# A hybrid decoder block: four edits where the retention stage begins

## The chip, the core and the metric

The kernel runs on one core of one Trainium2 chip. A core has a tensor engine for matrix products (PE, with its weight loads shown apart as PEld), a vector engine (DVE), a scalar engine (ACT), GpSimd (POOL), and a queue engine (SP) that mostly issues DMA transfers. Each engine works through its own list of instructions in order; semaphores order the engines among themselves. The metric is device time in microseconds (us). The kernel before took 2226.19 us, the median of three runs (2223.69 to 2228.32).

## The reference

One decoder block for one sequence of 1024 tokens of width 1024, all in float32:

```python
mod = jax.nn.silu(c) @ w_ada[l] + b_ada[l]
sh1, sc1, g1, sh2, sc2, g2 = jnp.split(mod, 6, axis=-1)
h = modulate(rms_norm(x, norm1_g[l]), sh1, sc1)
x = x + g1[:, None, :] * token_mixer(h, ...)
h = modulate(rms_norm(x, norm2_g[l]), sh2, sc2)
x = x + g2[:, None, :] * squared_relu_mlp(h, w_ff1[l], w_ff2[l])
return rms_norm(x, norm_f_g)
```

The token mixer projects `h` to queries, keys, values and gates. One branch is a chunkwise retention with 4 heads (256 channels for queries and keys, 512 for values) over 8 chunks of 128 tokens:

```python
s = jnp.einsum('bhid,bhjd->bhij', qi, ki) * inner_decay[None]
o = (jnp.einsum('bhij,bhje->bhie', s, vi)
     + jnp.einsum('bhid,bhde->bhie', qi, state) * q_decay[None, :, :, None])
state = (state * chunk_decay[None, :, None, None]
         + jnp.einsum('bhjd,bhje->bhde', ki * k_decay[None, :, :, None], vi))
```

Its output is normalized per head, scaled, multiplied by `silu(rg)` and projected. The other branch is a dilated sliding-window attention. The two are merged by sigmoid gates and projected once more.

## The kernel before, in words

Every product is made in float32 by splitting each operand into a high part and a low part and summing three matmuls (`mm3`, lines 201, 203 and 205: low weights by high data, high by low, high by high). So a product has the shape "128 by 128 weights, 128 by 512 data, three times". ACT usually makes the high part (a copy) and DVE the low part (a subtraction).

The stages follow each other: modulation and first norm; the attention values (`av`); queries, keys and gates (`queries_keys`); the retention values (`values`); retention (`chunk`, once per head and chunk, 32 times); attention; the output projections; the MLP. What surrounds the change is the end of `values`, the first chunks of retention, and the opening of attention.

**Values.** `values` goes through 14 steps of four parts `p`. Each part's matmuls are followed, one part later, by `v_post`, which finishes a result on ACT and DVE and stores it to device memory (`vd`, line 1070). The last but one step makes the tiles `vo12p` (lines 1061 and 1062), the last makes `vr1p` (lines 1066 to 1068; `vr10`, `vr11`, `vr12`, `vr13` by part). In the last but one step `values` also prepares the first two chunks' rotated queries and keys, `jit_qk(0)` and `jit_qk(1)`, and calls `ahead(2)` once. In the last step POOL queues eight reloads of halves of `hh` and `hl` (lines 1099 and 1100). Then it opens retention's memory (`open_ret`) and fetches values and queries and keys of the next two chunks.

**Retention.** A chunk `g` has these parts, in this order on PE: the score product `sT` and the transposes `kT` (`s_kt`, made one chunk ahead, the first two in chunk 0), the state's increments `kv` (two, from `kh`, `kl` and the values), the output `o` (from the state's halves `sh`, `sl` and the scores), the transposes `oT` of the previous chunk's normalized output, and between them pieces of the gate projection `rg`. `s_kt` copies the scores out with ACT into a small tile `sm` (line 638), multiplies by the decay and splits them (lines 639 to 642), then makes `kh` and `kl` (lines 648 and 649). The state is updated on DVE (lines 703 and 705) and split into `stateh` and `statel` (lines 719 and 720). `o` is normalized on DVE with a detour over POOL (`bn`, `ba`, `gr`, `onm`, lines 729 to 735); `onm` is the last reader of `o`. `jit_qk(i)` splits the fetched queries and keys of chunk `i` into `j`: a copy on ACT (line 615) and a subtraction on POOL (line 616). The products other than `rg` rotate over four banks of PSUM, so that a new product waits for the last reader of an earlier one; `kT` of the third chunk, for one, takes the bank of the first chunk's `o`.

**Loads in order.** `Steps` holds a list of steps, each with loads that a helper turns into operands. Loads are issued on SP in the order of the list, at most three ahead of those used, into three buffers `raw`. `ahead(n)` prepares the loads of the following step: `split_w` for weights (lines 191 and 192), and `mod_prep` for one column of the later modulations (a DVE product with a sum, line 455, and an addition, line 457). Each chunk's step holds one modulation load, each second one a weight load before it.

**Memory.** The pools are stacks: a pool opened where another was closed lies on the same bytes, and within a pool each kind of tile gets its place when its first tile is made. A new tile waits for the last users of whatever lay on its bytes, DMA stores among them. Retention's pool lies on the pool of the stages before, which has 26 tiles of 4 KB for each partition. Its kinds are the state, then values `V`, queries and keys `qk`, the small tiles `sm`, `smh`, `sml`, `kh`, `kl`, the split operands `j`, the tiles `bn` to `on`, and the 12 tiles of 4 KB of the kind "E" (`etile`, line 524), which hold each head's transposed outputs `on{h}{e}` and gates `srg{h}{e}`. Before the change the first E tile is made in `on_T` in chunk 1, so the E tiles lie behind all others.

**The opening of attention.** In `att_step(0, 0)` the last head is finished: `u_final` (line 663) scales each of its four `on` tiles on ACT (line 670), multiplies by `srg` on DVE (line 672) and stores to `y` (line 673). `result_sums` queues sums of `y` on POOL. Then `open_att` closes retention's pool and opens attention's, on the same bytes. `q_prep` makes `qh` and `ql` (lines 1209 and 1210) and `k_split` makes `kh` and `kl` of the first attention head from the projection `ak` (lines 1218 and 1219); the scores `sc` need all four, and stand on PE between pieces of the next `ak`:

```python
hi, lo = ring(f"kh{pair}{g}{a}"), ring(f"kl{pair}{g}{a}")
src, h_, l_ = by_blocks(ps, g), shaped(hi, g), shaped(lo, g)
nc.scalar.copy(h_, src)
nc.vector.tensor_sub(l_, src, fv(h_))
```

Of the kernel before, what the change touches and what calls it, by code (L numbers as in the profile page):

```python
# [134 lines left out]
def block_kernel(ctx, tc, io, stop=None, dbg=None):  # L135
# [3 lines left out]
    def fv(t):  # L139
        return t.bitcast(F32)  # L140
# [56 lines left out]
    def mm3(outs, w, xs, first, last, skip=False):  # L197

        wh, wl = w
        for o, (xh, xl) in zip(outs, xs):  # L200
            nc.tensor.matmul(o, wl, xh, start=first, stop=False, skip_group_check=skip)  # L201
        for o, (xh, xl) in zip(outs, xs):
            nc.tensor.matmul(o, wh, xl, start=False, stop=False, skip_group_check=skip)  # L203
        for o, (xh, xl) in zip(outs, xs):
            nc.tensor.matmul(o, wh, xh, start=False, stop=last, skip_group_check=skip)  # L205
# [246 lines left out]
    def mod_prep(i):  # L452

        def prep(raw):
            nc.vector.scalar_tensor_tensor(raw, raw, 1.0, cb, op0=ALU.mult, op1=ALU.mult,
                                           accum_out=mods[:, i:i + 1])
            nc.vector.tensor_add(mods[:, i:i + 1], mods[:, i:i + 1], vec[:, VC_BADA + i:VC_BADA + i + 1])
        return prep

    def mod_load(i):  # L460
        return io["w_ada"][i], mod_prep(i)
# [19 lines left out]
    def proj_mm(ps, w, ks=range(NK)):  # L481
        outs = ps if isinstance(ps, list) else [ps[:, 0, :], ps[:, 1, :]]
        for k in ks:
            mm3(outs, wk(w, k), hx[k], k == 0, k == NK - 1)
# [32 lines left out]
    def open_ret():  # L517
# [3 lines left out]
        R["sh"] = R["p"].tile([P, 2, DV], F32R, name="stateh")  # L521
        R["sl"] = R["p"].tile([P, 2, DV], F32R, name="statel")

    def etile(name, dt=F32):
        return R["p"].tile([P, 1024], dt, tag="E", bufs=12, name=name)

# [54 lines left out]
    hd = {}  # L581
    NG = H * NC
# [25 lines left out]
    def jit_qk(i):  # L608
        src = hd["qk", i]
        if i > 1:  # L610
            t = R["p"].tile([P, 2, 4, C], F32R, tag="j", bufs=2, name=f"j{i}")
        else:
            t = whl.tile([P, 1024], F32R, tag=("wh", "wl")[i], name=f"j{i}")
            t = t.rearrange("p (a b c) -> p a b c", a=2, b=4)
        nc.scalar.copy(t[:, 0], src)  # L615
        nc.gpsimd.tensor_sub(t[:, 1], src, fv(t[:, 0]))  # L616
        hd["j", i] = t

    def s_kt(i):

        p = R["p"]
        g = i
        h, c = divmod(g, NC)
        t = hd["j", g]
        ps = ps_s(f"sT{h}{c}")
        for i in range(2):
            nc.tensor.matmul(ps[:, :2 * C], t[:, 0, 2 + i, :], t[:, :, i, :], start=i == 0, stop=False,
                             skip_group_check=True)
            nc.tensor.matmul(ps[:, :C], t[:, 1, 2 + i, :], t[:, 0, i, :], start=False, stop=i == 1,  # L629
                             skip_group_check=True)  # L630
        pk = ps_s(f"kT{h}{c}", (P, 2, P)) if c < NC - 1 else None
        if pk is not None:
            for i in range(2):
                nc.tensor.transpose(pk[:, i, :], hd["qk", g][:, 2 + i], ident)
        sm = p.tile([P, C], F32, tag="sm", bufs=1, name=f"sm{h}{c}")
        smh = p.tile([P, C], F32R, tag="smh", bufs=2, name=f"smh{h}{c}")
        sml = p.tile([P, C], F32R, tag="sml", bufs=2, name=f"sml{h}{c}")
        nc.scalar.copy(sm, ps[:, :C])  # L638
        nc.vector.tensor_add(sm, sm, ps[:, C:2 * C])
        nc.vector.tensor_mul(sm, sm, decay[:, h * C:(h + 1) * C])  # L640
        nc.scalar.copy(smh, sm)
        nc.vector.tensor_sub(sml, sm, fv(smh))
        hd["s", g] = (smh, sml)
        if pk is not None:
            kd = ct[:, CS_KDEC + h:CS_KDEC + h + 1]
            kh = p.tile([P, 2, P], F32R, tag="kh", bufs=1, name=f"kh{h}{c}")
            kl = p.tile([P, 2, P], F32R, tag="kl", bufs=1, name=f"kl{h}{c}")
            nc.scalar.mul(kh, pk, kd)
            nc.vector.scalar_tensor_tensor(flat(kl), flat(pk), kd, fv(flat(kh)), op0=ALU.mult, op1=ALU.subtract)
            hd["k", g] = (kh, kl)  # L650

    def on_T(h, c):

        po = ps_s(f"oT{h}{c}", (P, 4, P))
        on = hd["o", h, c]
        if c == 0:
            hd["on", h] = [etile(f"on{h}{e}") for e in range(4)]
        for e in range(4):
            nc.tensor.transpose(po[:, e, :], on[:, e * P:(e + 1) * P], ident)
        for e in range(4):  # L660
            nc.scalar.copy(hd["on", h][e][:, c * C:(c + 1) * C], po[:, e, :])
# [13 lines left out]
    def chunk(h, c, ahead, w=None):  # L675
        p = R["p"]
        g = NC * h + c
        if g + 3 < NG:
            fetch(g + 3)
        if c % 2 == 0:  # L680
            hd["rgw"] = w
            hd["rgp"] = ps_mm(f"rg{h}{c}")

        ks = {0: (5, 6, 6), 1: (6, 7, 8)}.get(g) or [4 * (c % 2) + i for i in (0, 2, 4)]
        if g == 0:
            proj_mm(hd["rgp"], hd["rgw"], range(2))
            s_kt(0)
            proj_mm(hd["rgp"], hd["rgw"], range(2, 5))
        vh, vl = hd["v", g][:, 0], hd["v", g][:, 1]
        st, sh, sl = R["state"], R["sh"], R["sl"]  # L690
        kvs = []
        if c < NC - 1:
            kh, kl = hd["k", g]
            for i in range(2):
                kv = ps_s(f"kv{h}{c}{i}")
                mm3([kv], (kh[:, i, :], kl[:, i, :]), [(vh, vl)], True, True)
                kvs.append(kv)
        if g == 0:
            s_kt(1)
        proj_mm(hd["rgp"], hd["rgw"], range(*ks[:2]))  # L700
        for i, kv in enumerate(kvs):
            if c == 0:
                nc.vector.tensor_copy(st[:, i, :], kv)
            else:
                nc.vector.scalar_tensor_tensor(st[:, i, :], st[:, i, :], float(GAMMA[h] ** C), kv,
                                               op0=ALU.mult, op1=ALU.add)
        if g > 0:
            ahead(2)
        if 0 < g < NG - 1:
            s_kt(g + 1)  # L710
        po = ps_s(f"o{h}{c}")
        if c > 0:
            t = hd["j", g]
            for i in range(2):
                mm3([po], (t[:, 0, i, :], t[:, 1, i, :]), [(sh[:, i, :], sl[:, i, :])], i == 0, False)
        mm3([po], hd["s", g], [(vh, vl)], c == 0, True)
        if c < NC - 1:
            for i in range(2):
                nc.scalar.copy(sh[:, i, :], st[:, i, :])
                nc.vector.tensor_sub(sl[:, i, :], st[:, i, :], fv(sh[:, i, :]))  # L720
        if g + 2 < NG:
            jit_qk(g + 2)
        if g > 0:
            on_T(*divmod(g - 1, NC))
        proj_mm(hd["rgp"], hd["rgw"], range(*ks[1:]))
        bn = p.tile([P, 6], F32, tag="bn", bufs=2, name=f"bn{h}{c}")
        ba = p.tile([P, 2], F32, tag="ba", bufs=2, name=f"ba{h}{c}")
        gr = p.tile([P, 1], F32, tag="gr", bufs=2, name=f"gr{h}{c}")
        nc.vector.bn_stats(bn, po)
        nc.vector.bn_aggr(ba, bn)  # L730
        nc.vector.tensor_scalar(gr, ba[:, 1:2], ct[:, CS_QD2 + h:CS_QD2 + h + 1], GN_EPS, op0=ALU.mult, op1=ALU.add)
        nc.gpsimd.tensor_tensor(gr, gr, mhalf[:, 0:1], op=ALU.pow)
        nc.vector.tensor_mul(gr, gr, ct[:, CS_QD + h:CS_QD + h + 1])
        on = p.tile([P, DV], F32, tag="on", bufs=1, name=f"onm{h}{c}")
        nc.vector.tensor_scalar(on, po, ba[:, 0:1], gr, op0=ALU.subtract, op1=ALU.mult)
        hd["o", h, c] = on
        if g == 0:
            ahead(2)
        if c % 2 == 1:
            hd["srg", h, c // 2] = etile(f"srg{h}{c // 2}")  # L740
            nc.scalar.activation(hd["srg", h, c // 2], flat(hd["rgp"]), AF.Silu)
        if h > 0 and c < 4:
            u_final(h - 1, (c,))

    def wsplit(ap):
        return ap, split_w
# [368 lines left out]
    later_mods = [G1 + k for k in range(NK)] + [SH2 + k for k in range(NK)] + \  # L1115
                 [SC2 + k for k in range(NK)] + [G2 + k for k in range(NK)]

    for h in range(H):
        for c in range(NC):
            steps.add((lambda h, c: lambda ahead, *w: chunk(h, c, ahead, *w))(h, c),  # L1120
                      ([wsplit(io["w_rg"][4 * h + c // 2])] if c % 2 == 0 else []) + [mod_load(later_mods[8 * h + c])],
                      manual=True)


# [1334 lines left out]
```

## Time and profile before

| what | value |
|---|---|
| median of three runs | 2226.19 us (2223.69 to 2228.32) |
| the profiled execution | 2226.56 us; span from first to last instruction 2224.8 us |
| PE busy | 2177.1 us (98%) |
| DVE, ACT, POOL busy | 1454.5 us (65%), 907.3 us (41%), 145.5 us (7%) |
| mean granted clock of PE | 0.997 |
| bytes moved by DMA | 408.93 MB, 184 GB/s over the span |

The profile is one execution on the chip. Its page gives busy times by engine, the span in 40 slices, the chain of work that ended last, and groups of instructions. The trace behind it can be asked for the instructions of a stretch in order of time, for who waited for whom, and for busy times in windows. A row of the timeline has the start and the duration in us, the engine, the line of the kernel, the operation, the tile written and the tiles read, the shapes, a count where equal instructions were merged, and in brackets the idle time of the engine before it with what ended it. Matmuls are pipelined: the next one starts before the one before has ended. SPq is SP's queue; a DMA is shown at its issue, and its landing comes later. A view of the DMAs in a stretch lists issues with their sizes and the median us from issue to landing.

### The profile page before, as it was taken

The page shows a single profiled execution, that of the slowest core. Times are in us where ns is not written, and L with a number is a line of the kernel's source. Part 1 is how long each engine was busy: PE and PEld are TensorE (multiplying, and loading weights), DVE is VectorE, ACT ScalarE, POOL GpSimd, SP SyncE. Part 2 cuts the span into 40 slices and gives each one's busy share as a digit, 9 for nine tenths or more (in the row PEclk, how much of TensorE's full clock was granted, in tenths as well). Part 3 has the DMA queues.
Part 4 walks back from the last instruction along what each step waited for, and adds up shares of the span by engine and source line. Part 5 has one row for each costly group of instructions (what it writes and reads, how often), then busy time and mean ns, then how long its engine had stood idle before and what let it go on. Part 6 is the DMA issues. An engine that isn't in the chain of part 4 may idle for free.

```text
span 2224.8 us, 27161 instructions
## 1 busy us (share of the span) xinstructions
PE 2177.1 (98%) x10130; PEld 1803.4 (81%) x10130; DVE 1454.5 (65%) x2285; ACT 907.3 (41%) x1665; POOL 145.5 (7%) x168
## 2 busy tenths in 40 slices
PE   7999999999999999999999999999999999999998
PEld 4888888888877888888888788888778888888887
DVE  6628777764448778855554644676876665787855
ACT  4323332223434445544534633424454445533412
POOL 0001111000012122100000000002100000000003
PEclk9999999999999999999999999999999999999999
DMA  9539999725775556549813355645144444745322
GB/s 364 200 134 284 299 284 284 200 103 189 250 268 169 167 179 212 188 162 248 235 60 96 105 196 211 237 160 176 62 149 152 149 156 168 261 139 171 122 85 77
DMA packets 154371, 408.93 MB, mean 184 GB/s; under 512 B 27062, under 2 KB 54973, under 8 KB 149822
## 3 DMA queue, kind: packets, MB, share of 16 engines
q1 hardware_dynamic: 148542, 363.14, 46.5%
q0 software_dynamic: 5696, 44.04, 8.4%
q8 instruction: 80, 1.31, 0.2%
q14 instruction: 53, 0.43, 0.1%
HBM read 316.27 MB, written 156.13 MB: 212 GB/s over the span
## 4 chain that ended last, share of the span: by engine, by line
PE 86%; DVE 6%; ACT 3%; DMA 2%; issue 1%; POOL 0%; SPq 0%; POOLq 0%; DVEq 0%; ACTq 0%
PE qap L203 5%; PE qap L201 5%; PE qap L205 5%; PE av L769 4%; PE fp L203 4%; PE fp L201 4%; PE fp L205 4%; PE rg L201 2%; PE rg L203 2%; PE rg L205 2%; PE f2a L203 2%; PE f2a L201 2%; PE f2a L205 2%; PE ak L201 2%; PE ak L203 2%; PE ak L205 2%
## 5 line engine op out<-in xcount | busy, mean ns | idle before, releaser
L201 PE MATMUL qap<-hh,qaw 128*128 128x512 f32 x216 | 84.0, 389 | 0.0
L203 PE MATMUL qap<-hl,qaw 128*128 128x512 f32 x216 | 84.0, 389 | 0.0
L205 PE MATMUL qap<-hh,qaw 128*128 128x512 f32 x216 | 84.0, 389 | 0.0
L616 POOL TENSOR_TENSOR j<-qk,j 128x512 fp32r<-128x512 f32 x32 | 43.3, 1352 | 465.0 <-ACT j L615 465.0
L1918 ACT ACTIVATE a<-a 128x512 f32<-128x512 f32 x48 | 30.3, 632 | 76.2 <-DVE a L1917 76.2
L1272 ACT ACTIVATE P<-P,ng 128x128 f32<-128x128 f32 (+1 forms) x96 | 41.9, 438 | 39.2 <-DVE ng L1269 39.2
L258 DVE TENSOR_TENSOR fw<-w1r,fw 128x512 fp32r<-128x512 f32 x48 | 33.0, 688 | 37.6 <-ACT fw L248 37.6
L1815 POOL TENSOR_TENSOR accnf<-accnf,sqnf 128x256 f32<-128x256 f32 (+1 forms) x18 | 16.6, 922 | 613.5 <-ACT sqnf L1814 613.4
L258 DVE TENSOR_TENSOR qaw<-wa,qaw 128x512 fp32r<-128x512 f32 x54 | 36.0, 685 | 30.9 <-ACT qaw L248 30.9
L2104 ACT CAST w2h<-w2s 128x512 fp32r<-128x512 f32 x36 | 22.4, 621 | 78.1 <-DVE w2s L2142 77.0
L201 PE MATMUL fp<-h2h,fw 128*128 128x512 f32 x128 | 50.0, 390 | 0.0
L203 PE MATMUL fp<-h2l,fw 128*128 128x512 f32 x128 | 49.8, 389 | 0.0
L205 PE MATMUL fp<-h2h,fw 128*128 128x512 f32 x128 | 49.8, 389 | 0.0
L201 PE MATMUL roa<-rh,rwl 128*128 128x512 f32 x128 | 49.8, 389 | 0.0
L203 PE MATMUL roa<-rl,rwh 128*128 128x512 f32 x128 | 49.8, 389 | 0.0
L205 PE MATMUL roa<-rh,rwh 128*128 128x512 f32 x128 | 49.8, 389 | 0.0
L1653 DVE TENSOR_TENSOR rwl<-rwl,rwh 128x1024 fp32r<-128x1024 f32 x25 | 30.2, 1221 | 29.1 <-ACT rwh L1683 29.1
L638 ACT COPY sm<-sT 128x128 f32<-128x128 f32 x32 | 8.5, 266 | 98.8 <-PE sT L629 92.7
L201 PEld LDWEIGHTS qap<-hh,qaw 128*128 128x128 f32 x216 | 40.5, 188 | 8.5
L205 PEld LDWEIGHTS qap<-hh,qaw 128*128 128x128 f32 x216 | 40.5, 188 | 8.4
L203 PEld LDWEIGHTS qap<-hl,qaw 128*128 128x128 f32 x216 | 40.5, 188 | 8.4
L1815 POOL TENSOR_TENSOR accn<-accn,sqn 128x512 f32<-128x512 f32 x12 | 15.5, 1294 | 478.5 <-ACT sqn L1814 478.5
(3081 smaller groups left out, 7181.0 us busy)
## 6 DMA issues: line engine op xcount, KB each, us to landing
v<-vd SPq DMA_DIRECT2D x32, 512.0 KB, 4.9
raw<-in_w_ada_dram SPq DMA_DIRECT2D x32, 512.0 KB, 4.9
w1r<-in_w_ff_dram SPq DMA_DIRECT2D x32, 512.0 KB, 5.0
vd<-vo SPq DMA_DIRECT2D x24, 512.0 KB, 6.5
yt<-y POOLq DMA_DIRECT2D x6, 2048.0 KB, 15.3
xsd<-as SPq DMA_DIRECT2D x24, 512.0 KB, 2.7
w2r<-in_w_ff2s_dram SPq DMA_DIRECT2D x24, 512.0 KB, 7.6
em<-in_w_ada_dram SPq DMA_DIRECT2D x16, 512.0 KB, 10.2
```

The source lines that it names most:

```text
L201: nc.tensor.matmul(o, wl, xh, start=first, stop=False, skip_group_check=skip)
L203: nc.tensor.matmul(o, wh, xl, start=False, stop=False, skip_group_check=skip)
L205: nc.tensor.matmul(o, wh, xh, start=False, stop=last, skip_group_check=skip)
L258: nc.vector.tensor_sub(t[:, 512:], src, fv(t[:, :512]))
L616: nc.gpsimd.tensor_sub(t[:, 1], src, fv(t[:, 0]))
L638: nc.scalar.copy(sm, ps[:, :C])
L769: nc.tensor.matmul(av[g][c], x[k][:, c * C:(c + 1) * C], w[j][:, ws], start=k == 0 and (x, j) == parts[0], stop=k == NK - 1 and (x, j) == ...
L1272: nc.scalar.activation(v, v, AF.Exp, bias=ng[:, blk:blk + 1], accum_out=st[:, g, blk, 2 + a:3 + a])
L1653: nc.vector.tensor_sub(lo, fv(lo), fv(hi))
L1815: (nc.vector if f == 7 else nc.gpsimd).tensor_add(G["acc", key], G["acc", key], sq)
L1918: nc.scalar.activation(o, o, AF.Relu)
L2104: nc.scalar.copy(hi, src)
```

## The change

Four edits, all around the entry of retention. `open_ret` makes the four `on` tiles of head 0 at once, right after the state, and `on_T` no longer makes them for head 0; since these are the first tiles of the kind "E", all 12 E tiles get their place there, ahead of `V`, `qk` and the small tiles. `jit_qk(2)`, which splits the third chunk's rotated queries and keys, is called in chunk 0 right after `s_kt(1)` and not behind the split of the state. The second modulation's load moves from the step of chunk 1 into that of chunk 0, so that `ahead(2)` in `values` prepares both first modulations. In chunk 0 `ahead(2)` is called where all other chunks call it; the next step then holds nothing to prepare.

```diff
@@ open_ret
+        hd["on", 0] = [etile(f"on0{e}") for e in range(4)]
+
@@ on_T
-        if c == 0:
+        if c == 0 and h > 0:
             hd["on", h] = [etile(f"on{h}{e}") for e in range(4)]
@@ chunk
         if g == 0:
             s_kt(1)
+            jit_qk(2)
         proj_mm(hd["rgp"], hd["rgw"], range(*ks[:2]))
...
-        if g > 0:
-            ahead(2)
+        ahead(2)
         if 0 < g < NG - 1:
             s_kt(g + 1)
...
-        if g + 2 < NG:
+        if 0 < g < NG - 2:
             jit_qk(g + 2)
...
         hd["o", h, c] = on
-        if g == 0:
-            ahead(2)
@@ the steps of retention
-                      ([wsplit(io["w_rg"][4 * h + c // 2])] if c % 2 == 0 else []) + [mod_load(later_mods[8 * h + c])],
+                      ([wsplit(io["w_rg"][4 * h + c // 2])] if c % 2 == 0 else []) +
+                      [mod_load(later_mods[8 * h + i]) for i in ({0: (0, 1), 1: ()}.get(8 * h + c, (c,)))],
```

## The prediction

> **The bound.** I read the page, then the waits of the tensor engine, then its timeline where the waits are long.
>
> ```profile
> span 2224.8 us, 27161 instructions
> PE 2177.1 (98%) x10130; PEld 1803.4 (81%) x10130; DVE 1454.5 (65%) x2285; ACT 907.3 (41%) x1665; POOL 145.5 (7%) x168
> ...
> PE 86%; DVE 6%; ACT 3%; DMA 2%; issue 1%; POOL 0%; SPq 0%; POOLq 0%; DVEq 0%; ACTq 0%
> ```
>
> The tensor engine (PE) is busy for 98% of the span and carries 86% of the chain that ended last. A change pays only where PE stands still or runs slowly, and costs only where it makes PE wait. This is the entry of retention in PE's timeline (start, duration, in brackets the idle time before and its releaser):
>
> ```profile
> 661.83 0.61 PE L205 MATMUL rg<-hh,raw_4661h 128*128 128x512 f32 x2
> 664.65 0.54 PE L201 MATMUL kv<-v,kl 128*128 128x512 f32 x1 [2.21 <-DVE kl L649]
> 674.03 0.39 PE L627 MATMUL sT<-j 128*128 128x256 f32 x1 [0.70 <-POOL j L616]
> 675.66 0.44 PE L634 MATMUL kT<-ct,qk 128*128 128x128 f32 x2 [0.95 <-DVE onm L735]
> 677.59 0.50 PE L201 MATMUL o<-stateh,j 128*128 128x512 f32 x1 [1.49 <-DVE state L705]
> 683.20 0.39 PE L201 MATMUL kv<-v,kl 128*128 128x512 f32 x1
> ```
>
> Four stalls, 5.35 us together, between 662.44 (661.83 + 0.61) and the third chunk's first kv at 683.20. The same stretch cut into windows of 3.41 us (busy us and count of PE, PEld, DVE, ACT, POOL, then PE's granted clock, DMA share, GB/s):
>
> ```profile
> 661.55:664.97 3.42, 1.21 (x5) 0.69 (x5) 1.36 (x4) 0.94 (x3) 0.00 (x0) 1.00 1.04 392
> 664.97:668.38 3.41, 3.41 (x13) 2.90 (x12) 0.00 (x0) 0.26 (x1) 0.00 (x0) 0.50 0.80 274
> 671.79:675.21 3.42, 2.22 (x11) 1.47 (x9) 2.62 (x7) 2.05 (x4) 1.86 (x2) 1.00 0.00 0
> 675.21:678.63 3.42, 1.49 (x7) 1.07 (x8) 3.38 (x7) 0.00 (x0) 0.00 (x0) 1.00 0.14 25
> 678.63:682.04 3.41, 3.41 (x12) 2.73 (x11) 2.89 (x8) 0.88 (x3) 0.00 (x0) 0.50 1.03 375
> ```
>
> After a window with PE busy 1.21 or 1.49 us the next is granted half the clock; after one with 2.22 us it is not. A half-speed window full of matmuls loses 3.41 / 2 = 1.7 us. So the entry holds 5.35 + 3.4 = 8.8 us that are not work; that is all a perfect entry could give.
>
> **Small tiles.** The first stall ends with the first chunk's `sm`, on whose chain `kl` and kv hang:
>
> ```profile
> 662.46 0.27 ACT L638 COPY sm<-sT 128x128 f32<-128x128 f32 x1 [6.13 <-DMA vd<-vr]
> 664.12 0.48 DVE L649 SCALAR_TENSOR_TENSOR kl<-kT,ct,kh 128x256 fp32r<-128x256 f32 x1
> ...
> 654.36 8.00 DMA vd<-vr
> ...
> 648.92 8.48 SPq L1070 DMA_DIRECT2D vd<-vr  x4
> ...
> DMA packets 3525, 8.02 MB, mean 388 GB/s; under 512 B 325, under 2 KB 1163, under 8 KB 3523
> ...
> raw<-in_w_ada_dram SPq DMA_DIRECT2D x1, 512.0 KB, 9.3
> ```
>
> `sm` lies where `vr12` lay, whose store (third of four) is issued at 654.36 and lands 8.00 us later. With `on00` to `on03` allocated first, the twelve E tiles come ahead of the small ones, and `sm` lies on `vr10`, the first store, issued at 648.92. A 512 KB load issued 3.5 us before it took 9.3 us, so the first store takes 8.0 to 9.3 and lands at 656.9 to 658.2. From 645.3 to 666 the DMA engines are full (388 GB/s), and the change puts another 512 KB into that (with the modulation): 524 KB / 388 = 1.35 us, up to 2.0 while the reloads of `hh` share the engines. I take the late end, 660.2. `sm` at 660.3 is 2.16 earlier, `kl` ends at 664.60 - 2.16 = 662.44, just when PE is ready: kv at 662.5 instead of 664.65, and no half-speed window behind it. Bounds: nothing, if `vr10` lands as late as `vr12` did; 2.2 + 1.7 = 3.9 at most.
>
> **Third chunk.** `j2` moves ahead of the copies of the state. The rows that set the pace:
>
> ```profile
> 670.17 1.28 DVE L703 COPY state<-kv 128x512 f32<-128x512 f32 x2
> 671.54 1.30 DVE L720 TENSOR_TENSOR statel<-state,stateh 128x512 fp32r<-128x512 f32 x2
> 672.00 0.61 ACT L615 CAST j<-qk 128x512 fp32r<-128x512 f32 x1
> 672.70 1.28 POOL L616 TENSOR_TENSOR j<-qk,j 128x512 fp32r<-128x512 f32 x1 [22.94 <-ACT j L615]
> 674.79 0.81 DVE L735 TENSOR_SCALAR onm<-o,ba,gr 128x512 f32<-128x512 f32 x1
> 675.52 1.22 DVE L455 SCALAR_TENSOR_TENSOR raw<-raw,cb 128x1024 f32<-128x1024 f32 x1
> 676.85 1.28 DVE L705 SCALAR_TENSOR_TENSOR state<-state,kv 128x512 f32<-128x512 f32 x2
> 681.87 0.48 DVE L649 SCALAR_TENSOR_TENSOR kl<-kT,ct,kh 128x256 fp32r<-128x256 f32 x1
> 658.05 0.55 SPq L597 DMA_DIRECT2D qk<-qkd  x1
> qk<-qkd SPq DMA_DIRECT2D x1, 256.0 KB, 7.7
> ```
>
> At full speed two rg take 0.61 and one kv 0.39, so matmuls of 512 columns start 0.22 to 0.23 us apart, six in 1.36. Then kv runs from 662.5 to 663.9, and sT with kT, two such matmuls' columns in six pieces, to about 664.4. From `sm` to the end of `kl` is 664.60 - 662.46 = 2.14: the second `kl` ends at 666.6, the copies of the state at 667.8. PE does rg and o until 666.5, the second kv pair until 668.0, rg until 669.4. `qk02` lands at 658.05 + 7.7 + 1.35 = 667.1, `j2` ends on ACT at 667.7 and on POOL at 669.0: sT at 669.4 no longer waits. That removes the 0.70, and if `qk` is late it costs nothing until 667.5.
>
> But kT needs the bank of `o`, so it waits for `onm`, whose chain is untouched. ACT is held by `j2` until 667.7 and makes `stateh` by 668.3. Then `statel` meets `j2` on POOL, and there are rows for such a meeting: POOL's op beside a VectorE subtraction of two SBUF operands that otherwise takes 1.21.
>
> ```profile
> 637.18 1.21 DVE L1027 TENSOR_TENSOR vwl<-vwl,vwh 128x1024 fp32r<-128x1024 f32 x1
> 639.85 1.29 POOL L616 TENSOR_TENSOR j<-qk,j 128x512 fp32r<-128x512 f32 x1 [0.30 <-ACT j L615]
> 639.90 2.31 DVE L1027 TENSOR_TENSOR vwl<-vwl,vwh 128x1024 fp32r<-128x1024 f32 x1
> ```
>
> It took 2.31, so I let `statel` start when POOL ends, at 669.0 (0 to 1.1 us for this meeting; 0.7 taken). The Trainium skill, page "SBUF — State Buffer", section "SBUF: two separate sides", says that the pair of ports shared by VectorE and GpSimd is an exclusive lock held for a whole instruction; these rows agree. From the start of `statel` to the end of `onm` is 675.60 - 671.54 = 4.06: 673.1. kT starts at 673.15: its stall grows from 0.95 to about 3.2.
>
> **Modulation.** The second modulation (DVE 675.52 to 676.85, 1.33 us, between `onm` and `state`) moves into the values' stage. There it stands before one `vo`, whose store goes out 1.3 later; `v01` now lies on that tile and waits for the store on SP, behind the `vr` stores that are issued until 657.4 anyway, and the queue stays deep enough to hide up to 1 us of a later issue. The matmuls of the last values' step take nothing from it; were that cover gone, it would cost its 1.33. Once it has run, its buffer is free, and the load of a later modulation, 512 KB, goes out in the values' stage instead of in the first chunks: the extra transfer costed above, and one load less on SP in the first chunk. So L705 follows `onm` directly: first half done at 673.75, o at 673.8 instead of 677.59. The third chunk's `kl` ends 681.87 + 0.48 - 676.85 = 5.50 after L705 starts (673.05): 678.55. PE needs 683.20 - 677.59 = 5.61 from o to kv with a half-speed window in it, 5.61 - 1.7 = 3.9 without. The stall of 3.2 will most likely bring one: kv at 679.4; without, it waits for `kl`: 678.6. The entry gives 683.20 - 679.4 = 3.8 us (3.8 to 4.6; with the bounds above 0 to 5.2). Nothing takes it back before the exit, for PE is busy all the way there, at full clock:
>
> ```profile
> 684.00:989.00 305.00, 305.00 (x1481) 253.58 (x1480) 238.70 (x492) 145.93 (x357) 55.49 (x60) 1.00 0.53 175
> ```
>
> **The exit.** When attention opens, its tiles lie on retention's memory from the bottom up. The E tiles were at the top, out of the way; now they are at the bottom. In the changed program `kh010` lies on `on33`, the last tile of retention, and its copy on ACT carries a new wait, on the store of `on33`; before it lay on an old `v`.
>
> ```profile
> 986.32 1.23 DVE L672 TENSOR_TENSOR on<-on,srg 128x1024 f32<-128x1024 f32 x1 [0.18 <-ACT on L670]
> 983.35 4.58 SPq L673 DMA_DIRECT2D y<-on  x4
> 987.13 1.00 ACT L1218 CAST kh<-ak 128x1024 fp32r<-128x1024 f32 x1
> 988.60 1.22 DVE L1219 TENSOR_TENSOR kl<-ak,kh 128x1024 fp32r<-128x1024 f32 x1
> 989.87 0.38 PE L203 MATMUL sc<-kl,qh 128*128 128x256 f32 x1 [0.35 <-DVE kl L1219]
> ...
> y<-on SPq DMA_DIRECT2D x4, 512.0 KB, 2.8
> ```
>
> The store is issued when DVE ends, 987.55, and takes 2.8 or, as the queue fills behind it, a little more: it lands at 990.5. `kh` runs to 991.6, `kl` to 992.9, and PE's second sc starts at 992.95 instead of 989.87: 3.1 us lost (2.8 to 4), since sc waits for `kl` today. Behind `kh` on ACT stand the split of the next weights and the next `qh`; both have a projection's time to spare. PE is idle for 3.4 of 3.8 us, more than the entry's stalls, so I add one half-speed window, 1.7 (0 to 3.4). Sum 4.8. The Trainium skill, "TensorE: Matmul & The Clock Gate", section "What's actually happening", lets the clock fall after an idle window of about 3.4 us; the table agrees on the length, but not that the window must be idle throughout. By this page of the Trainium skill neither stall need bring a half-speed window, and the sum would be -4.6 + 3.1 = -1.5.
>
> **Sum.** -3.8 + 4.8 = +1.0. Their phase is chance, so I weigh in a little of the case without half-speed windows (-4.6 + 3.1 = -1.5) and take +0.7. The profiled execution took 2226.56 us (span 2224.8), 0.37 above the median of the runs, 2226.19: 2226.9 for the median.
>
> **Rivals.** (a) Only the entry counts: the wait of `kh` is hidden, because the store of `on33` lands before ACT comes to `kh`. Then -3.8 to -5.2: 2221.0 to 2222.4. It decides if the store lands by 987.2; against it, the store is issued at 987.55.
>
> (b) Slower: the entry's gain is lost to the DMA queue. Place: `qk02`, `j2`, `stateh`, `statel`, `onm`, one behind the other. Each us that `qk02` lands after 667.1 moves `onm` and o by one; at 670.9 the 3.8 us are gone and the exit's 4.8 stand alone: 2231.0. For it: the queue is full, and 7.7 to 9.3 us deep. Against it: only 512 KB are added, 1.35 us.
>
> (c) The change does not do what it says: `sm` meets another late store and kv stays at 664.65. Then `onm` stays at 675.6, only the 1.3 us of the modulation are won, and the exit costs 4.8: +3.5, 2229.7. Against it: `vr10` is issued 5.4 us before `vr12`.
>
> (d) No half-speed window follows either stall: -1.5, 2224.7. For it: 2.22 busy us in a window did not bring one. Against it: 1.49 did, and both new stalls leave less than that in most positions of the window. The Trainium skill's page on the clock gate, named above, would expect this one.
>
> **Numbers.** The forecast has 0.56, (d) 0.10, (c) 0.05: all within 0.2% (4.5 us, about what a measurement of this kernel can tell from no change). (a) has 0.15; two thirds of it lie beyond -0.2%, 0.10. (b) has 0.14, of which 0.13 beyond +0.2%. Hence faster 0.10, same 0.77, slower 0.13. The likeliest case alone reaches from 2223.5 to 2229.5 (the runs shown spread from 2223.69 to 2228.32); leaving about 0.1 out on each side, 2221.9 to 2230.8.
>
> **Signs.** Right: ACT's `sm` about 2 us earlier and no long wait before the first kv; kT waiting about 3 us for `onm`; the third chunk's kv about 4 us earlier; `kh` (L1219 in the changed file) waiting for the DMA y<-on, a stall of about 3 us before sc, and half clock behind it. Wrong: sc without a stall (a), `j` waiting for `qk` past 668 (b), a first kv at 664.65 (c), full clock throughout (d).

## The result

The changed kernel took 2232.41 us, the median of eight runs (2231.58 to 2234.39); the kernel before took 2226.28 beside it (2223.69 to 2228.87). The ratio is 1.0029, with a 95% interval of 1.0020 to 1.0039: slower by 6.1 us, where 2226.9 had been predicted. The time lies outside the predicted range. The profiled execution took 2232.31 us.

The page of the changed kernel (span, busy time of PE, shares of the chain that ended last):

```profile
span 2230.5 us, 27163 instructions
...
PE 2177.7 (98%) x10130; PEld 1804.1 (81%) x10130; DVE 1455.0 (65%) x2285; ACT 906.5 (41%) x1665; POOL 145.3 (7%) x168
...
PE 84%; DVE 6%; DMA 3%; ACT 3%; issue 1%; POOL 0%; SPq 0%; POOLq 0%; DVEq 0%; ACTq 0%
```

PE's work is the same (2177.7 against 2177.1 us busy). The span is 5.7 us longer, so nearly all of the loss is PE standing still. The page does not say where. The timeline does, read beside the kernel before. First the entry and the exit in the changed kernel:

```profile
660.49 0.27 ACT L640 COPY sm<-sT 128x128 f32<-128x128 f32 x1 [4.30 <-DMA vd<-vr]
662.68 0.50 PE L201 MATMUL kv<-v,kl 128*128 128x512 f32 x1 [0.37 <-DVE kl L651]
672.60 0.44 PE L636 MATMUL kT<-ct,qk 128*128 128x128 f32 x2 [2.18 <-DVE onm L737]
673.29 0.47 PE L201 MATMUL o<-stateh,j 128*128 128x512 f32 x1 [0.25 <-DVE state L708]
678.01 0.50 PE L201 MATMUL kv<-v,kl 128*128 128x512 f32 x1 [0.57 <-DVE kl L651]
978.13 4.58 SPq L675 DMA_DIRECT2D y<-on  x4
985.58 1.01 ACT L1219 CAST kh<-ak 128x1024 fp32r<-128x1024 f32 x1 [3.56 <-DMA y<-on]
986.64 0.39 PE L201 MATMUL sc<-kh,ql 128*128 128x256 f32 x1 [2.46 <-ACT kh L1219]
987.90 0.39 PE L203 MATMUL sc<-kl,qh 128*128 128x256 f32 x1 [0.87 <-DVE kl L1220]
```

The third chunk's kv starts at 678.01 instead of 683.20, and the retention's last stores start at 978.13 instead of 983.35: 5.2 us gained, and kept all through retention. At the exit 2.46 + 0.87 = 3.33 us of stalls stand where there were 0.35; the second sc is still 2.0 us earlier than before (987.90 against 989.87). Up to here the prediction's rows come out, without its half-speed windows: this execution has none at the entry or the exit. What the prediction does not have stands 65 us later, in the attention:

```profile
1050.89 1.05 ACT L191 CAST raw_8402h<-raw 128x1024 fp32r<-128x1024 f32 x1 [4.17 <-DMA raw<-in_w_gate_dram]
1053.35 0.71 PE L201 MATMUL gate<-hh,raw_8402l 128*128 128x512 f32 x2 [0.69 <-DVE raw_8402l L192]
1055.82 1.05 ACT L191 CAST raw_8501h<-raw 128x1024 fp32r<-128x1024 f32 x1 [3.88 <-DMA raw<-in_w_gate_dram]
1058.87 0.36 PE L201 MATMUL sc<-kh,ql 128*128 128x256 f32 x1 [1.18 <-DVE P L1250]
1061.63 0.58 PE L203 MATMUL sc<-kl,qh 128*128 128x256 f32 x1 [2.41 <-DVE kl L1220]
1085.18 0.73 PE L201 MATMUL gate<-hh,raw_8603l 128*128 128x512 f32 x2 [1.01 <-ACT g00s L1539]
```

The weights of two gate projections come late, ACT and DVE fall behind, and PE waits 0.69 + 1.18 + 2.41 = 4.28 us, with a half-speed window (1061.11 to 1064.52) behind it. Before the change, the splits of the same two weights on ACT and the wait of the last row stood here:

```profile
1048.90 1.03 ACT L191 CAST raw_8402h<-raw 128x1024 fp32r<-128x1024 f32 x1
1050.10 1.05 ACT L191 CAST raw_8501h<-raw 128x1024 fp32r<-128x1024 f32 x1 [0.17 <-DMA raw<-in_w_gate_dram]
1080.89 0.73 PE L201 MATMUL gate<-hh,raw_8603l 128*128 128x512 f32 x2 [0.79 <-ACT g00s L1538]
```

So 2.0 us ahead at 988 have become 4.3 behind at 1085. The other 1.4 us of the 5.7 come later; a half-speed window at 1293.21, which the profile of the kernel before does not have, loses about 1.7 there. Why the weights are late is seen in the issues on SP and POOL. Before, where `std<-st` writes 16 KB of the attention's statistics to device memory, `stn<-std` reads them back, and `yt` are the sums of results that `result_sums` puts on POOL's queue:

```profile
989.64 0.60 POOL L566 DMA_DIRECT2D yt<-y  x1 [17.06 <-DMA y<-on]
1022.70 0.62 SPq L1330 DMA_DIRECT2D std<-st  x1
1023.65 1.17 POOL L567 DMA_DIRECT2D yt<-y  x1 [20.78 <-DMA yt<-y]
1027.17 0.37 SPq L1331 DMA_DIRECT2D stn<-std  x1
1028.95 12.10 SPq L85 DMA_DIRECT2D raw<-in_w_gate_dram  x2
```

And after:

```profile
984.40 0.60 POOL L568 DMA_DIRECT2D yt<-y  x1 [17.04 <-DMA y<-on]
1017.72 1.17 POOL L569 DMA_DIRECT2D yt<-y  x1 [20.65 <-DMA yt<-y]
1019.43 0.62 SPq L1331 DMA_DIRECT2D std<-st  x1
1038.39 0.37 SPq L1332 DMA_DIRECT2D stn<-std  x1
1039.48 0.86 SPq L85 DMA_DIRECT2D raw<-in_w_gate_dram  x2
```

The sums start with the retention's last stores, so they came 5.2 us earlier (984.40 against 989.64). The statistics follow the attention, which has lost part of the gain at the exit, and came only 3.3 us earlier (1019.43 against 1022.70). Before, the write left 0.95 us ahead of the next sum; after, it leaves 1.71 us behind it. It then takes 19 us instead of 4.4 until the read can be issued, SP waits for it, and the gate's two loads queued behind are issued at 1039.48 and 1039.95 instead of 1028.95 and 1036.60: 10.5 and 3.4 us later.

### The profile page after: what moved, and what is told of

The parts are those of the page before. It is cut to its first block, busy times and chain, and to the rows that moved or that the text cites. A ratio compares the mean times of both kernels' runs of the same rounds, so it can differ in the third digit from the quotient of the medians.

```text
span 2230.5 us, 27163 instructions
## 1 busy us (share of the span) xinstructions
PE 2177.7 (98%) x10130; PEld 1804.1 (81%) x10130; DVE 1455.0 (65%) x2285; ACT 906.5 (41%) x1665; POOL 145.3 (7%) x168
## 4 chain that ended last, share of the span: by engine, by line
PE 84%; DVE 6%; DMA 3%; ACT 3%; issue 1%; POOL 0%; SPq 0%; POOLq 0%; DVEq 0%; ACTq 0%
PE qap L203 5%; PE qap L205 5%; PE qap L201 5%; PE av L769 4%; PE fp L201 4%; PE fp L203 4%; PE fp L205 4%; PE rg L201 2%; PE rg L203 2%; PE rg L205 2%; PE f2a L203 2%; PE f2a L205 2%; PE f2a L201 2%; PE ak L201 1%; PE ak L203 1%
## 6 DMA issues: line engine op xcount, KB each, us to landing
em<-in_w_ada_dram SPq DMA_DIRECT2D x16, 512.0 KB, 10.2
```

## The experiments

All times are medians, with the kernel before measured beside them; "difference" is taken from that median, the ratio is that of the runs.

| kernel | us | difference | ratio (95%) |
|---|---|---|---|
| the change | 2232.41 | +6.13 | 1.0029 (1.0020 to 1.0039) |
| 1: ring behind | 2223.95 | -2.23 | 0.9990 (0.9981 to 0.9999) |
| 2: statistics read later | 2229.49 | +3.31 | 1.0012 (1.0003 to 1.0021) |
| 3: placement alone | 2233.60 | +7.42 | 1.0030 (1.0019 to 1.0040) |
| 4: without the placement | 2227.71 | +1.53 | 1.0003 (0.9994 to 1.0012) |
| 5: sums 100 us later | 2228.56 | +2.68 | 1.0008 (0.9999 to 1.0017) |
| 6: before, sums 100 us later | 2225.83 | -0.05 | 0.9995 (0.9985 to 1.0004) |
| 7: ring behind, sums 100 us later | 2223.41 | -2.47 | 0.9984 (0.9975 to 0.9993) |
| 8: ring behind, old modulations | 2223.55 | -2.33 | 0.9986 (0.9976 to 0.9995) |
| 9: ring behind alone | 2223.74 | -3.17 | 0.9988 (0.9979 to 0.9998) |
| 10: ring behind alone, sums later | 2223.78 | -3.13 | 0.9984 (0.9976 to 0.9993) |
| 11: ring behind, old modulations, sums later | 2223.49 | -3.42 | 0.9986 (0.9977 to 0.9995) |
| 12: the change, sums 4 us later | 2228.63 | +2.01 | 1.0012 (1.0003 to 1.0021) |

**1. The exit stall taken away.** The ring of twelve E tiles is made behind `V` and `qk`. The small tiles then lie at the same place as with the change, and what lies under the attention's first tiles is `V` and `qk` again.

```diff
-        hd["on", 0] = [etile(f"on0{e}") for e in range(4)]     (in open_ret)
         open_ret()
         for g in (1, 2):
             fetch(g)
+        hd["on", 0] = [etile(f"on0{e}") for e in range(4)]
```

> The change in full, but the ring of twelve is taken behind the tiles of the values and of queries and keys instead of ahead of them: the first chunk's small tiles stay where the change puts them, and the attention's first tiles lie where values and queries lay, as before the change. Theory (the 3.3 us exit stall on the last store, and through it the statistics' write that falls behind a sum of results, make the whole loss): the entry keeps its gain of 5.1 us, the exit stall of 3.3 us goes, the statistics' write leaves the chip again before the next sum starts, and the stalls at 1052 to 1064 us are gone: 2221.2 us, between 2220.5 and 2223 with a half-speed window more or less. Rival (the entry's gain itself, by bringing the attention 5 us forward, upsets its loads): the exit stall goes alone, about 2228 to 2229 us. Rival (the two half-speed windows are the matter, the rest is noise): about 2227 us.

Measured 2223.95 us: the loss is gone and a gain is left, but 2.2 us and not 5. The trace has no exit stall (0.36 us), the write of the statistics leaves at 1017.56, ahead of the sum at 1018.41, and there is no stall at 1050 to 1064. Its profiled run (2229.59, the slowest of eleven) has waits of 2.21 and 3.78 us at 1077.72 and 1082.20, behind a later gate weight for which ACT waits 5.35 us. The other ten times lie between 2222.51 and 2225.66 and do not bear this out; why that weight was late is left open.

**2. The read of the statistics later.** SP is not held; the slow write stays.

```diff
-        nc.sync.dma_start(A["stn"][:, g], natural(d, 0, 4))
+        A["std", g] = d
+        for x in {(0, 1): (), (0, 2): (1, 2)}.get((pair, g), (g,)):
+            nc.sync.dma_start(A["stn"][:, x], natural(A["std", x], 0, 4))
```

> The changed kernel, with the read of the first group's statistics (stn, 16 KB) issued together with that of the second group, 26 us later, so that SP isn't held by it ahead of the gate's weights; the write of the statistics stays where it falls. Theory (SP held by the read behind a slow write makes the gate's weights late): the exit stall of 3.3 us stays, the stalls at 1052 to 1061 us and the window behind them go; against the kernel before, 5.2 gained at the entry, 3.0 lost at the exit: 2224.0 us, 2225.7 with the window at 1293 us. Rival (it is the sums' traffic that makes the weights late, whatever SP does): no change, 2230 to 2233 us.

Measured 2229.49 us. By the time alone this is nearer the rival, so the trace has to decide (issues on SP; the write landed 16.8 us later):

```profile
1021.79 0.63 SPq L1331 DMA_DIRECT2D std<-st  x1
1024.00 0.33 SPq L85 DMA_DIRECT2D raw<-aqd  x1
1025.14 11.71 SPq L85 DMA_DIRECT2D raw<-in_w_gate_dram  x2
```

The write is as slow as in the changed kernel, the first of the gate's loads is issued 14 us earlier (1025.14 against 1039.48), and no stall stands between 1050 and 1064: the mechanism is as expected. The time is still 3.8 to 5.5 us above the theory's. In the profiled run a half-speed window at the exit (989.45 to 992.86), which the changed kernel's did not have, and waits of 0.73, 0.76 and 0.69 us in the MLP (from 1905) make up for part of it. Of these waits the changed kernel's profile has one, of 0.62 us; why the others come is not shown.

**3. The placement alone.** Only the first part of the diff (`open_ret` and `on_T`) is applied to the kernel before.

```diff
+        hd["on", 0] = [etile(f"on0{e}") for e in range(4)]
...
-        if c == 0:
+        if c == 0 and h > 0:
```

> The kernel before with the first part alone: the ring of twelve taken first. Theory: the first chunk comes 2.2 us sooner, the exit stall of 3.3 us is there in full, the attention runs 1 us late while the sums run 2 us early, so the statistics' write falls behind a sum and the stalls of some 6.5 us follow: 2226.3 - 2.2 + 3.0 + 6.5 = 2233.6 us, 2232 to 2236 with windows. Rival (the loss needs the whole of the entry's gain): 2226.3 - 2.2 + 3.0 = 2227.1 us.

Measured 2233.60 us, as the theory had it, but its terms do not come out in the trace (2231.24, the fastest of the eight). The entry gains 4 us and not 2.2 (the third chunk's kv at 679.05 against 683.20). The exit has the stall and two half-speed windows (987.49 to 994.32). The late weights make PE wait for 0.62, 0.18 and 2.35 us, with one half-speed window at 1086.48, which is about 3 us more than before and not 6.5. So the exact number is partly luck. What it does show is the order. The sum comes 5.1 us ahead of the statistics' write here (rows of SP; on POOL the sum is issued at 1017.83), and the read waits 15 us:

```profile
1022.97 0.62 SPq L1332 DMA_DIRECT2D std<-st  x1
1037.71 0.38 SPq L1333 DMA_DIRECT2D stn<-std  x1
```

**4. Without the placement.** The other edits without the first: both `etile` lines of experiment 3 are as in the kernel before.

```diff
-        hd["on", 0] = [etile(f"on0{e}") for e in range(4)]
...
-        if c == 0 and h > 0:
+        if c == 0:
```

> The changed kernel without its first part: the rotated operands sooner and the modulations in the values' stage, with the small tiles and the ring where they were before. Theory: no exit stall, sums and attention move together, nothing behind the entry changes: the entry's gain less the 2.2 us of the placement, 5.2 - 2.2 = 3.0: 2223.3 us, between 2222 and 2225 as a half-speed window in the entry stays or goes. Rival (a gain at the entry upsets the attention by itself): over 2227 us. Rival (without the earlier small tiles the other two parts are worth nothing, since the first chunk's wait sets the rest): 2226 us.

Measured 2227.71 us: the theory's 2223.3 is wrong. The number is the first rival's (over 2227), but the trace does not show its reason: the write leaves ahead of the sum (1021.53 against 1022.88), and no stall stands at 1050 to 1064. By the mechanism the second rival is nearest: the entry itself gives next to nothing (the third chunk's kv at 682.37 against 683.20), since the first chunk's `sm` waits longer than before (ACT; before 662.46):

```profile
664.27 0.27 ACT L638 COPY sm<-sT 128x128 f32<-128x128 f32 x1 [7.91 <-DMA vd<-vr]
```

What this profile loses behind the entry is a wait of 1.57 us for a gate (0.79 before) and a half-speed window at 1288.60.

**5. The sums 100 us later.** The sums are first read at 1314.8 us, so they can wait.

```diff
-                result_sums()                                   (in att_step)
...
             nc.scalar.activation(t, flat(ps), AF.Sigmoid)       (in cover_step)
+            if (pair, n) == (0, 1):
+                nc.gpsimd.tensor_copy(t[:, 0:1], t[:, 0:1])
+                result_sums()
```

> The changed kernel with the sums of results (yt, 16 MB through POOL's queue) begun some 100 us later: POOL first copies one column of the second gate's tile onto itself, and so waits for that gate, at about 1085 us. Theory (it is the sums' traffic that the statistics' write and, behind it, the gate's weights run into): the exit stall of 3.3 us stays, the statistics are back within some 5 us, and no weight is late at 1050 to 1064: 2226.2 - 5.1 + 3.3 = 2224.4 us, 2223 to 2226 with windows. Rival (the loads at 1050 us are late for another reason, such as the order of SP's queue): 2230 to 2233 us.

Measured 2228.56 us: 3.85 less than the change. The trace shows the read 3.8 us behind the write (1024.24 and 1020.46) and no late weight; the rival is out. It is 4.2 us above the expectation of 2224.4 and outside its range: by 7, below, the exit's price is 1.9 us higher than the 3.3 put down, and the entry's gain is 2.4 us instead of 5.1.

**6 and 7. The same on the kernel before, and with the ring behind.** The edit of 5 on the kernel before and on that of experiment 1:

```diff
-                result_sums()
...
+                nc.gpsimd.tensor_copy(t[:, 0:1], t[:, 0:1])
+                result_sums()
```

> The kernel before with the sums of results begun 100 us later in the same way, to price what the sums cost there. Theory (before the change the statistics' write just slips between two sums): only the small waits for gate weights go, 0.2 and 0.8 us: 2225.4 us, 2224 to 2227. Rival (the sums cost the attention several us whatever their place against the statistics): 2222 us or less.

> The change with the ring behind the tiles of the values (no exit stall) and the sums begun 100 us later. Theory (exit stall and the clash with the sums are together the whole loss): the entry's gain alone is left, 4 to 5 us of it, as the first small tiles' store is late by 0.4 to 1.2 us: 2221.5 us, 2220 to 2223. Rival (the sums hurt as much where they are put): as the run with the ring behind alone, 2224 us.

Before the change the place of the sums is worth nothing that can be measured (2225.83 against 2225.88), and with the ring behind at most 0.5 us (2223.41 against 2223.95), against 3.85 us in the changed kernel (3.45 by the differences of the table). So the sums cost only where the exit has moved the statistics behind one of them. The four kernels make a square, the sums early or late, the exit stall there or not:

| | exit stall | no exit stall |
|---|---|---|
| sums where they were | 2232.41 | 2223.95 |
| sums 100 us later | 2228.56 | 2223.41 |

Without the clash the ring in front costs 2228.56 - 2223.41 = 5.15 us, which I put down to the exit. It is not the exit alone: the entry differs too, with the third chunk's kv at 679.07 in the profile of 5 and at 680.01 in that of 7. The expectation of 2221.5 for 7 was too low by 1.9, and the time is nearer to its rival's 2224: the entry's gain is 2.4 us against 6, not 4 to 5.

**8. The modulations where they were,** with the ring behind:

```diff
-        ahead(2)
+        if g > 0:
+            ahead(2)
...
+        if g == 0:
+            ahead(2)
...
-                      [mod_load(later_mods[8 * h + i]) for i in ({0: (0, 1), 1: ()}.get(8 * h + c, (c,)))],
+                      [mod_load(later_mods[8 * h + c])],
```

> The change with the ring behind the tiles of the values, and the modulations where they were before (one in each of the first two chunks, the first chunk's behind its output): small tiles elsewhere and third chunk's operands sooner alone. Theory (the third chunk's wait is set by the length of DVE's work in the first chunk, and the modulation is 1.5 to 2 us of it): 1.7 us more than with the modulations moved: 2225.7 us. Rival (the operands sooner carry all of the third chunk's gain): 2224 us.

Measured 2223.55 us, no more than with the modulations moved (2223.95, 2223.41): the theory's 2225.7 is out, the rival is right, and the move is worth nothing. Its row of ACT says why:

```profile
658.22 0.27 ACT L638 COPY sm<-sT 128x128 f32<-128x128 f32 x1 [2.03 <-PE kT L634]
```

With the old modulations `sm` follows the score product at once; the store of `vr10` is out of the way. With the move `sm` waits for that store until 660.49 (the change) to 661.76 (experiment 7). What the third chunk gains, the first has paid. The store is late because of the load that the moved modulation lets go: two of 512 KB instead of one right before the `vr` stores, which then take 9.2 us instead of 6.5 in the median (the DMAs between 640 and 662, changed kernel):

```profile
vd<-vr SPq DMA_DIRECT2D x4, 512.0 KB, 9.2
...
raw<-in_w_ada_dram SPq DMA_DIRECT2D x2, 512.0 KB, 9.3
```

**9, 10 and 11. Less of the change.** The ring behind alone (as experiment 1, without the other parts), the same with the sums later, and experiment 8 with the sums later:

```diff
         for g in (1, 2):
             fetch(g)
+        hd["on", 0] = [etile(f"on0{e}") for e in range(4)]
...
-        if c == 0:
+        if c == 0 and h > 0:
```

> The kernel before with one part alone, in its other form: the ring of twelve taken behind the tiles of the values, so that the first chunk's small tiles lie on the first stored tile and no tile of the attention lies on the ring's last stores. Theory (the earlier small tiles are the whole gain of the entry): the first kv without a stall at 662.0 us, all else of the entry as before, no exit stall, no late statistics: as the run with the operands sooner too, 2223.5 us, 2222.5 to 2224.5. Rival (the third chunk's operands sooner carry part of it): 2224.5 to 2225.5 us.

> The same with the sums of results begun 100 us later. Theory (with the ring behind, the statistics' write slips between two sums as before the change, so that the sums cost little): within 0.7 us of the run with the ring behind alone, 2223 us. Rival (where the sums stand costs 2 us or more in any case): 2221.5 us or less.

> Small tiles elsewhere with the ring behind, third chunk's operands sooner, modulations where they were, and the sums of results begun 100 us later. Theory: the entry's gain of 2.3 us by the medians and 0.5 us from the sums: 2223.0 us, 2222 to 2224. Rival (moving the modulations is worth something once nothing else disturbs): over 2224 us, above the 2223.4 us of the run that moves them.

Measured 2223.74, 2223.78 and 2223.49 us, all as the theory has it. In 9 the first kv does not wait, while the third chunk has its old stalls:

```profile
670.15 0.39 PE L627 MATMUL sT<-j 128*128 128x256 f32 x1 [0.72 <-POOL j L616]
671.77 0.44 PE L634 MATMUL kT<-ct,qk 128*128 128x128 f32 x2 [0.95 <-DVE onm L735]
673.70 0.51 PE L201 MATMUL o<-stateh,j 128*128 128x512 f32 x1 [1.49 <-DVE state L705]
```

The other two parts add nothing to it. The six kernels with the ring behind lie within 0.6 us of each other, 2.2 to 3.4 us below the kernel before: each beats both kernels, and 9 does it with one line added and one condition changed.

**12. The sums 4 us later.** The sharpest test of the place: everything of the change stays, and POOL waits for the attention's first `kl`.

```diff
             k_split(pair, g, a, ps)
+            if i == pair == 0:
+                nc.gpsimd.tensor_copy(A["st"][:, 0, 0:1, 0], fv(A["k", g, a][1])[:, 0:1])
+                result_sums()
```

> The changed kernel with the sums of results begun about 4 us later only: POOL first copies one column of the attention's first kl, and so starts at some 988.3 us instead of 984.4, as late against the attention as before the change, or a little more. Everything else, the full sums in the attention's first steps too, stays. Theory (what decides is whether the statistics' write, at 1019.4 us, leaves ahead of the next sum, which the change moved ahead of it to 1017.7): that sum starts at 1021.6 us, the statistics are back some 4 us after their write, and no weight is late at 1050 to 1064 us: as with the sums 100 us later, 2228.6 us, 2227 to 2229.5. Rival (the sums' traffic as a whole, not its place, makes the weights late): 2231 to 2233 us, with stalls at 1052 to 1064 us.

Measured 2228.63 us. The write left at 1022.72, 0.33 us ahead of the sum (POOL issues it at 1023.05), and the read followed 4.1 us later:

```profile
1022.72 0.62 SPq L1331 DMA_DIRECT2D std<-st  x1
1026.79 0.38 SPq L1332 DMA_DIRECT2D stn<-std  x1
1027.27 1.14 SPq L85 DMA_DIRECT2D raw<-aqd  x1
1028.50 12.40 SPq L85 DMA_DIRECT2D raw<-in_w_gate_dram  x2
```

No stall stands at 1050 to 1064. Some 5 us of delay for the sums (this one at 1023.05 against 1017.72) give the same 3.8 us as a hundred: it is the order of two issues that costs, not the traffic. The order is kept by 0.33 us only. The slowest of the eleven runs took 2234.92; whether the write fell behind in that one is not known, for only one was profiled.

## Why the prediction was wrong

The predicted sum was -3.8 at the entry, +4.8 at the exit, +1.0. By the runs it is -2.4 at the entry (7 against 6), +5.15 at the exit (5 against 7), and +3.85 by the clash (the change against 5): +6.6, where +6.1 was measured. That these three add up is no test, for they are steps from 2225.83 to 2232.41. The two profiles divide the loss otherwise: 5.2 us gained at the entry, 3.2 lost at the exit (to 2.0 ahead), 6.3 at the late weights (to 4.3 behind), 1.4 after them. The term that the prediction put at nothing is the largest loss in the profiles, and in the runs it is most of the miss.

**Small tiles: right.** `sm` was put at 660.3 and came at 660.49, kv at 662.5 and came at 662.68. The transfer of the moved load was costed at 1.35 to 2.0 us and costs the `sm` copy 2.3 us (660.49 against 658.22 in experiment 8; 661.76 in 7, 3.5).

**Third chunk: right in the rows, wrong in what they are worth.** kT was put at 673.15 and came at 672.60, o at 673.8 and came at 673.29, kv at 679.4 and came at 678.01, without the half-speed window that I had put in. The meeting of `statel` with `j` on POOL, put at 0.7 us, cost about 0.3: the two subtractions took 1.58 us together (L722) against 1.30. But the step "only the 1.3 us of the modulation are won" is wrong: without the placement (4) the moved load makes the first kv wait until 666.46, and with it nothing is won (8, 9). The prediction had charged the load to the small tiles and credited the modulation with its 1.33 us, and so did not see that the third part by itself is a loss at the first chunk.

**The exit: right in its stalls.** 3.1 us of stalls and one half-speed window of 1.7 were put down; 3.0 us of stalls are in the trace, and the price by the runs is 5.15. That the window comes is chance: the profiled run of the change had none, those of 2, 3 and 12 have one or two. The mean granted clock over all runs is 0.9964 in experiment 5 and 0.9979 in 7, and 0.0015 of 2222 us is 3.3 us, as much as two half-speed windows lose. But the profile of 5 has none at the exit; the window that it has and that of 7 has not stands at 1287.44. So it is not shown that windows at the exit make up the rest of the 5.15.

**The step that failed** is the one sentence on what follows the exit: "Behind `kh` on ACT stand the split of the next weights and the next `qh`; both have a projection's time to spare." It put what follows the exit at nothing; by the runs that costs 3.85 us. The queue behind the late instruction was followed on its own engine, to the next projection, and there the search ended. It should have been followed to the next thing on another queue that does not move with it. The sums on POOL start with the retention's stores and move with the entry's gain; the statistics move with the exit's loss; SP stands between them, and behind SP the weights. None of these is a wait at the place of the change, and so none of the rivals had it. Rival (b) named a DMA queue, but the one at the entry; it did not happen.

**Rivals.** (a) is out: the store landed after ACT came to `kh`. (c) is out as told (kv came at 662.68); experiment 4 has its entry without the exit, and cost 1.5 us where (c) put a gain of 1.3. (d) held in the profiled run of the change as far as the exit: no half-speed window followed either stall, and PE was 2.0 us ahead where (d) put 1.5. The loss came behind it all the same.

## What to carry to other kernels

A gain that moves one queue and a loss that moves another shift the two against each other, and the price can come tens of us later, where a small transfer leaves just behind a large one instead of just ahead. So beside the waits at the place of the change list what each moved queue meets downstream, and by how much it misses it now; here the margin between the two issues was 0.95 us. Where a large transfer is needed late (the sums, 330 us later), it can be moved at no cost (6), and one wait on POOL keeps it clear (5 and 7). To leave behind a sum does not cost by itself: the second group's write does so in the kernel before too (1048.07, behind a sum at 1045.96), its read follows 10.2 us later, and PE waits there no longer than in 5, where the sums are out of the way (0.79 us in both).

## What the runs showed of the hardware

**A small write beside a large sum.** The write of 16 KB landed after 4.4 us before the change, between two sums, and after 18.9 us when it was issued behind a sum of 2 MB. Between its issue and the read that waited for it, the DMA engines moved these (queues, packets, MB, share; the changed kernel, 1019.4 to 1038.4 us):

```profile
q0 software_dynamic: 320, 4.19, 84.7%
q1 hardware_dynamic: 1040, 0.02, 4.0%
```

The write is 1024 packets of 16 bytes, and the 4.19 MB on `q0` are the sum and the copy that follows it on POOL. From 1023.5 to 1029.5 us the two queues moved 158 and 147 packets, from 1029.5 to 1034.2 64 each, and then, with the 4.19 MB gone, `q1` moved 828 until 1038.4. Before the change `q0` moved 11 packets between the write's issue and the read's, and `q1` had 1047 packets through between 1023.5 and 1025.0. The Trainium skill, page "DMA: Bandwidth & Descriptors", section "Queues, rings and completion order", says that an engine goes round between the queues that have work, one packet at a time. The trace agrees: while both queues have work their packets go about one for one, so a write of many small packets is held to the pace of the large ones beside it.

**The clock's windows.** The half-speed windows of an execution lie on a grid of 3.413 us (1061.11 and 1293.21 in the changed kernel are 68 steps apart). Nearly all follow a window in which PE was busy for a short time. At the exit, in windows on the grid (busy us and count of PE first, granted clock behind the five engines), the changed kernel:

```profile
982.60:986.02 3.42, 1.58 (x7) 0.96 (x6) 0.86 (x1) 0.44 (x1) 0.60 (x1) 1.00 0.92 313
986.02:989.43 3.41, 1.91 (x10) 1.59 (x11) 2.81 (x3) 3.41 (x4) 0.00 (x0) 1.00 1.11 442
...
1057.70:1061.11 3.41, 0.36 (x1) 0.19 (x1) 3.41 (x7) 0.08 (x1) 0.00 (x0) 1.00 1.07 404
1061.11:1064.52 3.41, 2.88 (x9) 2.56 (x10) 2.76 (x4) 0.58 (x3) 0.00 (x0) 0.50 0.28 34
```

And experiment 2:

```profile
986.04:989.45 3.41, 1.35 (x8) 1.11 (x9) 2.24 (x2) 3.29 (x4) 0.00 (x0) 1.00 1.09 413
989.45:992.86 3.41, 3.41 (x10) 2.63 (x9) 2.38 (x3) 0.56 (x1) 0.00 (x0) 0.50 1.04 393
```

The same stall falls on the grid as 1.58 and 1.91, and costs no window, or as 1.35, and costs one. In the fourteen profiles every window, from 30 to 2200 us, with PE busy for 1.49 us or less is followed by half speed. From 1.53 to 1.67 us some are (1.61 at 661.82 in 12, 1.67 at 1595.66 in 9) and some are not (1.53 at the exit of 5, 1.64 at the entry of 7, 1.58 above). In experiment 3 two such windows follow each other; the first is busy for 2.51 us, but at half speed, which is 1.26 us of work. One stage does not fit: 2.5 to 2.6 us busy, in many short matmuls, with half speed behind it, ahead of 1293.21 in the changed kernel and at the same stage in 1, 4, 5, 8 and 12. So busy time is not the whole rule, and the rest is left open. The page "TensorE: Matmul & The Clock Gate" of the Trainium skill, section "What's actually happening", asks for an idle window; these windows were not idle.
